# A hybrid SSD and attention layer: the first unit of the gate z directly behind the first B block, with four of its eight groups as seven products, and the sums of weight pairs begun with the constants

## The chip, the core and the metric

The kernel runs on one core of a Trainium2 chip. The metric is the device time of one execution in microseconds (us). The engines are called as in the profile: PE is TensorE's matmuls, PEld its weight loads, DVE is VectorE, ACT is ScalarE, POOL is GpSimd, SP is SyncE. A name with a q behind it (SPq, POOLq, ACTq) is the DMA queue that the engine feeds.

## The reference

One layer with S = 256 tokens and D = 2048 features, all in fp32. Only the first projection and what hangs on it matter here:

```python
u = rmsnorm(h, norm_mix_pre)
proj = einsum('bsd,de->bse', u, w_in)
z, xbc, dt_raw, q, k, v = split(proj, IN_SPLITS)      # 2048 | 4096 | 32 | 2048 | 2048 | 2048 columns
xbc = silu(causal_depthwise_conv(xbc, conv_w, conv_b))
xs, bm, cm = split(xbc, (2048, 2048 + 1024))          # X, B, C
dt = softplus(dt_raw + dt_bias)
y = ssd_chunked(xh, dt, a, bm, cm) + d_skip * xh      # 8 groups of 4 heads
yg = y * silu(z)                                      # z is needed here, at the end of a group
y_ssm = yg * rsqrt(mean(yg * yg) + EPS) * ssm_norm_w
y_att = ...                                           # dilated attention from q, k, v
h = h + rmsnorm(concat(y_ssm, y_att) @ w_out, norm_mix_post)
h = h + rmsnorm(relu(rmsnorm(h, norm_mlp_pre) @ w_up) ** 2 @ w_down, norm_mlp_post)
```

## The kernel before, in words

**Products.** Every fp32 operand is taken apart into a high part (ACT copies it rounded, L147) and a low part (DVE subtracts, L148). A product is then three matmuls: high by high, high by low, low by high. The 16 blocks of 128 features of the sum over D are taken in eight groups of two, k = 0 to 7. For 512 columns of weights one group is one load of 512 KB (`fetch`, L152, issued by SP into one of four buffers `raw`), one split of 128x1024 into `hi` and `lo` (five buffers each), and its matmuls.

**Two ways to multiply.** A *feature block* (`gemm_features`, L491: the blocks B, C and X, with queries and keys of the attention) puts 512 output features on the partitions: L485 multiplies the high parts of the weights by both parts of the activations, 512 wide, and L488 the low parts by the high parts of the activations, 256 wide. A *unit* (`unit`, L451: z, and later most of the kernel) has the tokens on the partitions, and takes two blocks of 512 columns and both token blocks together. A *plain group* of a unit (`row_tile`, L331 to L333) is 24 matmuls of 128x512. A *seven* (`seven`, L386) multiplies the 2x2 blocks of a group with seven products in place of eight, 21 matmuls (L418 to L420). For that it adds weight blocks: DVE makes three sums of 128x512 (L252), and ACT and DVE split seven blocks (three of 128x1024, one of 128x512). The activations' sums for a k are made once by `sums_of_acts` (L368): four operations on DVE (L377 to L380) and a split into two places of `sh` and `sl`. There are eight such places, for four values of k. After the last seven, `combine_new` (L422) folds the seven products' banks together, with four operations on DVE. Inside a seven the adds and splits keep the order of the code on ACT and DVE.

**Sums of pairs.** One addend of a seven comes summed from DRAM. `next_pair` (L270) issues on POOL a copy of one weight block to a place in DRAM (L279) and a second transfer that adds another block to it (L280); the first use of each of the five places is preceded by a tiny write (L278) from `room["pairs"]`, which sets when the chain may begin. SP fetches the sum later (L156) into half of a `raw`. Four pairs run ahead (`PAIRS_AHEAD`).

**The order of the work.** `first_block` (L577) makes the first B block by hand. The loop at L883 to L898 then calls, in this order, C0, X0, the first z unit (`gates(0)`, L779), X1, then B1, C1, X2, the second z unit, X3. What is put into `waiting` is carried on a step at each `pump`: `first_conv` (L742), which waits three pumps and then spreads the reciprocal norm over the partitions (`over_partitions`, L639: `dg` on DVE at L644, a matmul at L645, a copy `rbc` at L646) and does the convolution of B; `steps` (L663), which loads the weights of dt through ACT's queue (L665), splits them into `wdt`, sets `room["pairs"]` from `wdt` (L668), starts the first four pairs, and makes dt and its cumulative sums; and the SSD groups (L800). A unit's first seven drains `waiting` first (L462). The reciprocal norm `rstd` itself is a power on POOL (L142). At its end a block B, C or X empties its four banks through ACT (L508) and DVE (L509). A z unit takes all eight PSUM banks, four of them those of `acc`. The first z unit has sevens for k = 1 and 3 (the plan at L433; k = 7 comes last and is plain).

The constants `cst` are loaded by SP at L547, behind the last load of the first block. The instructions of each engine run in the order in which a scheduler has put them when the program was built; inside `high_priority` they may go ahead of what stands earlier in the code, as far as the buffers allow.

Of the kernel before, what the change touches and what calls it, by code (L numbers as in the profile page):

```python
# [10 lines left out]
F32 = mybir.dt.float32  # L11
# [32 lines left out]
AHEAD = 1_000_000  # L44
# [11 lines left out]
PAIRS_AHEAD = 4  # L56
# [21 lines left out]
def hymba_layer(ctx: ExitStack, tc: tile.TileContext, x, norm_mix_pre, w_in, conv_w, conv_b, dt_bias, a_log,  # L78
# [24 lines left out]
    def u(k):  # L103

        t, i = us[k]
        return t[:, i]
# [16 lines left out]
    cst = fp.tile([P, consts.shape[1] - P], F32, name="cst")  # L123
# [8 lines left out]
    def bank():  # L132
        return pacc.tile([P, NB], F32, name="acc")

    def psmall():
        return psm.tile([P, NB], F32, name="ps")
# [7 lines left out]
    def split(hi, lo, src, scale=None):  # L144

        if scale is None:
            return (nc.scalar.activation(hi, src, AF.Copy),  # L147
                    nc.vector.tensor_tensor(lo, src, hi.bitcast(F32), op=ALU.subtract))  # L148
        return (nc.scalar.activation(hi, src, AF.Copy, scale=scale),
                nc.vector.scalar_tensor_tensor(lo, src, scale, hi.bitcast(F32), op0=ALU.mult, op1=ALU.subtract))  # L150
# [27 lines left out]
    room = {}  # L178
# [75 lines left out]
    pairs = []  # L254

    w_z, w_v, w_ups, w_downs = w_in[:, COL_Z:], w_in[:, COL_V:], [w_up[:, hf * 4096:] for hf in range(2)], [w_down, w_down[4096:]]
    orders = {}

    def order_of(ks, by_seven):
        return [(k, k in by_seven) for k in ks]  # L260

    def blocks_of(n):
        return n if isinstance(n, tuple) else (n * NB, (n + 1) * NB)

    def plan(name, src, n, order, by_seven):

        orders[name, n] = order_of(order, by_seven)
        pairs.extend((src, blocks_of(n), k) for k in order if k in by_seven)

    def next_pair():  # L270

        if not pairs:
            return
        src, (ca, c), k = pairs.pop(0)
        cb = slice(c, c + NB)
        d = places[len(paired) % len(places)]
        if len(paired) < len(places):
            nc.gpsimd.dma_start(d[:, 0:1], room["pairs"])  # L278
        nc.gpsimd.dma_start(d, src[k * KB * P:(k * KB + 1) * P, cb])  # L279
        nc.gpsimd.dma_start(d, src[(k * KB + 1) * P:(k * KB + 2) * P, cb], accum_op=ALU.add)  # L280
        paired.append((src, ca, k, d))
# [148 lines left out]
            nc.vector.tensor_tensor(b[0], more[1], u, op=ALU.add)  # L430
            nc.vector.tensor_tensor(b[1], more[3], b[0], op=ALU.add)

    plan("z", w_z, 0, (0, 2, 4, 6, 1, 3, 5), (1, 3))  # L433
    plan("z", w_z, 2, (0, 2, 1, 4, 3, 6, 5), (1, 3, 5))
    qk_blocks = [(COL_Q + hb * NB, COL_K + hb * NB) for hb in range(3)]
    plan("qk", w_in, qk_blocks[1], (0, 2, 1, 4, 3, 5, 6), QK_SEVENS)
# [226 lines left out]
    def steps():  # L663
        raw = sp1.tile([P, NK, 32], F32, name="raw_dt")
        nc.scalar.dma_start(raw, w_in[:, COL_DT:COL_DT + 32].rearrange("(k p) n -> p k n", p=P))  # L665
        wdt = sp1.tile([P, NK, 64], F32R, name="wdt")
        split(wdt[:, :, 0:32], wdt[:, :, 32:64], raw)
        room["pairs"] = wdt[:, 0, 32:33].bitcast(F32)  # L668
        with tc.high_priority(offset=AHEAD):
            for _ in range(PAIRS_AHEAD):  # L670
                next_pair()
        yield
        yield
        acc = psmall()
        for k in range(NK):
            nc.tensor.matmul(acc[:64, :S], wdt[:, k], u(k)[:, 0], start=k == 0, stop=False)
            nc.tensor.matmul(acc[:64, :S], wdt[:, k], u(k)[:, 1], start=False, stop=k == NK - 1)
        both = sp1.tile([64, S], F32, name="both")
        nc.vector.tensor_copy(both, acc[:64, :S])
        yield  # L680
        p = psmall()
        for t in range(NT):
            nc.tensor.matmul(p[:, t * 32:(t + 1) * 32], both[:, t * P:(t + 1) * P], two[:64], start=True, stop=True)
        with tc.high_priority(offset=AHEAD):
            y = sp1.tile([P, NT, 32], F32, name="dt_y")
            for t in range(NT):
                nc.vector.scalar_tensor_tensor(y[:, t], p[:, t * 32:(t + 1) * 32], rstd[:, t:t + 1], bias_b,
                                               op0=ALU.mult, op1=ALU.add)

            e = sp1.tile([P, NT, 32], F32, name="dt_e")  # L690
            nc.vector.scalar_tensor_tensor(e, y, -1.0, y, op0=ALU.mult, op1=ALU.min)
            nc.scalar.activation(e, e, AF.Exp)
            r = sp1.tile([P, NT, 32], F32, name="dt_r")
            nc.vector.tensor_scalar(r, e, 2.0, None, op0=ALU.add)
            nc.vector.reciprocal(r, r)
            s = sp1.tile([P, NT, 32], F32, name="dt_s")
            nc.vector.tensor_mul(s, e, r)
            q = sp1.tile([P, NT, 32], F32, name="dt_q")
            nc.vector.tensor_mul(q, s, s)
            h = sp1.tile([P, NT, 32], F32, name="dt_h")  # L700
            nc.vector.tensor_scalar(h, q, 2.0 / 17, None, op0=ALU.mult)
            for n in (15, 13, 11, 9, 7, 5, 3):
                nc.vector.scalar_tensor_tensor(h, h, 2.0 / n, q, op0=ALU.add, op1=ALU.mult)
            nc.vector.scalar_tensor_tensor(h, h, 2.0, s, op0=ALU.add, op1=ALU.mult)
            nc.vector.scalar_tensor_tensor(dt, y, 0.0, h, op0=ALU.max, op1=ALU.add)
            ea = sp1.tile([P, 32], F32, name="dt_a")
            nc.scalar.activation(ea, a_b, AF.Exp)
        yield
        with tc.high_priority(offset=AHEAD):
            for t in range(NT):  # L710
                nc.vector.scalar_tensor_tensor(dA[:, t], dt[:, t], -1.0, ea, op0=ALU.mult, op1=ALU.mult)
        for _ in range(7):
            yield
        p = psmall()
        for t in range(NT):
            nc.tensor.matmul(p[:, t * 32:(t + 1) * 32], triu, dA[:, t], start=True, stop=True)
        nc.tensor.matmul(p[:, 64:96], ones, dA[:, 0], start=True, stop=True)
        nc.vector.tensor_copy(acs.rearrange("p t h -> p (t h)"), p[:, 0:64])
        nc.scalar.activation(eacs, acs[:, 1], AF.Exp)
        nc.vector.tensor_sub(toend, p[:, 64:96], acs[:, 0])  # L720
        nc.scalar.activation(toend, toend, AF.Exp)
        p = psmall()
        for t in range(NT):
            nc.tensor.matmul(p[:32, t * P:(t + 1) * P], dA[:, t], triu, start=True, stop=True)
        rowed = sp1.tile([32, S], F32, name="rowed")
        nc.vector.tensor_copy(rowed, p[:32, :S])
        nc.scalar.dma_start(acs_d, rowed)
# [37 lines left out]
    def place_of_sums():  # L765

        room["sum"] = mp.tile([P, 4, S], F32, name="cT", bufs=5).rearrange("p (k f) s -> p k (f s)", k=KB)
# [11 lines left out]
    def gates(n):  # L779

        room["own"] = deque(mp.tile([P, NT, NB], F32, name="tk", bufs=3)[:, t] for t in range(NT))
        place_of_sums()
        room["sums"] = [v[:, k:k + KB] for k in range(NK // 2, NK, KB) for v in (sh, sl)]
        room["raw"], room["turn"], room["acts"] = [], 0, act_u
        gated = [mp.tile([P, NT, NB], F32, name="tk", bufs=3) for _ in range(2)]

        def end(b):
            def at_end(t, a):
                with tc.high_priority(offset=AHEAD):
                    v = gated[b][:, t]  # L790
                    nc.vector.tensor_tensor(v, a, v, op=ALU.subtract if b else ALU.add)
                    nc.scalar.activation(v, v, AF.Silu, scale=rstd[:, t:t + 1])
            return at_end

        more = [psmall(), bank(), psmall(), bank()]
        unit(w_z, n, orders["z", n], (7,), [bank() for _ in range(2 * NT)], more,
             lambda x: combine_new([[v[:, t] for t in range(NT)] for v in gated], x), 0, (end(0), end(1)))
        return gated
# [85 lines left out]
    zs = []  # L884
    for hb in range(2):
        bT = conv_block(COL_B + hb * NB, 16 + 4 * hb, first if hb == 0 else None)
        if hb == 0:
            waiting.append(steps())
        cT = conv_block(COL_C + hb * NB, 24 + 4 * hb)
        for xb in (2 * hb, 2 * hb + 1):  # L890
            xT = conv_block(COL_X + xb * NB, 4 * xb)
            if xb % 2 == 0:
                zs += gates(xb)
            for j in range(2):
                g = 2 * xb + j
                waiting.append(ssd_group(sp, g, bT[:, g % 4], cT[:, g % 4], xT[:, 2 * j:2 * j + 2],
                                         zs[xb][:, :, j * 256:(j + 1) * 256]))
# [659 lines left out]
```

## Time and profile before

| | us |
|---|---|
| three runs | 1453.19, 1455.0, 1452.5 |
| their median | 1453.19 |
| the profiled execution: first to last instruction (span) | 1451.4 |
| median less span: what lies outside the span | 1.8 |
| PE busy in the span | 1442.4 |
| DVE busy | 1300.4 |
| ACT busy | 947.1 |
| POOL busy | 162.3 |

A row of a timeline gives the start in us, the busy time of the group in us, the engine, the line, the operation, output and inputs, their shapes and the count; what stands in square brackets is the idle time ahead of it and what ended it. In a list of waits the three numbers are the time in all, the count and the longest. In a list of DMA issues the last number is the median time from the issue to the landing. Lines (L488) are those of the kernel before; in the kernel after, lines behind L667 stand four lower up to the loop, and one higher behind it (L753 is L749 after).

### The profile page before, as it was taken

Reading aid. Unit: us, or ns where it says so; the run is one execution under the profiler, and the core shown is the slowest. Engines: PE = TensorE matmul, PEld = TensorE weight load, DVE = VectorE, ACT = ScalarE, POOL = GpSimd, SP = SyncE. Lnnn points to the kernel's source line nnn. Section 1 sums busy time; section 2 is a strip of 40 time slices with the busy share of each in tenths; the row PEclk is TensorE's granted clock in tenths of the full one; section 3 lists DMA queues with packets and bytes.
Section 4 is the critical chain, followed back from the end, with each engine's and each line's share of the span. In section 5 each row is a group of like instructions: output and inputs, shape, how many; then the busy total and the mean of one; then the engine's idle time right before and its main releaser. Section 6 shows DMA issues by size and latency. Waiting matters only on the chain.

```text
span 1451.4 us, 20394 instructions
## 1 busy us (share of the span) xinstructions
PE 1442.4 (99%) x7042; PEld 1214.7 (84%) x7042; DVE 1300.4 (90%) x1881; ACT 947.1 (65%) x1351; POOL 162.3 (11%) x244
## 2 busy tenths in 40 slices
PE   9999999999999999999999999999999999999998
PEld 8888888888888888888888888888888888888886
DVE  7788888988999788689988999999889999999998
ACT  7577669665666666556657677656465776766664
POOL 0201110131111000010100011010111110101000
PEclk9999999999999999999999999999999999999999
DMA  8977656756898658588976798688888888788854
GB/s 267 272 219 222 189 175 187 239 170 195 231 253 248 196 127 244 173 270 257 280 225 217 210 311 240 203 221 251 249 255 279 255 245 247 210 293 265 248 179 160
DMA packets 172359, 332.97 MB, mean 229 GB/s; under 512 B 16048, under 2 KB 18976, under 8 KB 172256
## 3 DMA queue, kind: packets, MB, share of 16 engines
q1 hardware_dynamic: 144736, 272.37, 58.1%
q0 software_dynamic: 19648, 45.63, 15.7%
q10 hardware_dynamic: 7872, 13.68, 2.8%
q8 instruction: 55, 0.90, 0.3%
q14 instruction: 48, 0.39, 0.1%
HBM read 327.39 MB, written 49.84 MB: 260 GB/s over the span
## 4 chain that ended last, share of the span: by engine, by line
PE 76%; ACT 1%; DVE 1%; DMA 0%; issue 0%; ACTq 0%
PE acc L331 10%; PE acc L333 10%; PE acc L332 10%; PE acc L418 7%; PE acc L419 7%; PE acc L420 7%; PE acc L485 4%; PE ps L331 3%; PE ps L332 3%; PE ps L333 3%; PE ps L418 2%; PE ps L419 2%; PE ps L420 2%; PE acc L488 2%; PE acc L1463 1%; PE ps L938 0%
## 5 line engine op out<-in xcount | busy, mean ns | idle before, releaser
L148 DVE TENSOR_TENSOR lo<-raw,hi 128x1024 fp32r<-128x1024 f32 (+1 forms) x387 | 470.1, 1220 | 79.1 <-ACT hi L147 76.3
L147 ACT ACTIVATE hi<-raw 128x1024 fp32r<-128x1024 f32 (+1 forms) x387 | 404.2, 1050 | 204.2 <-PE acc L333 71.4
L485 PE MATMUL acc<-ua,hi 128*128 128x512 f32 x520 | 141.2, 401 | 0.1
L147 ACT ACTIVATE hi<-e 128x1024 fp32r<-128x1024 f32 x66 | 70.2, 1063 | 68.5 <-DVE e L252 62.7
L485 PEld LDWEIGHTS acc<-ua,hi 128*128 128x128 f32 x520 | 91.3, 189 | 14.2 <-ACT hi L147 0.2
L331 PE MATMUL acc<-hi,ua 128*128 128x512 f32 x228 | 90.6, 397 | 0.0
L332 PE MATMUL acc<-lo,ua 128*128 128x512 f32 x228 | 89.3, 392 | 0.0
L333 PE MATMUL acc<-hi,ua 128*128 128x512 f32 x228 | 89.2, 391 | 0.0
L331 PE MATMUL acc<-hi,sh 128*128 128x512 f32 x220 | 86.9, 395 | 0.0
L333 PE MATMUL acc<-hi,sl 128*128 128x512 f32 x220 | 85.8, 390 | 0.0
L332 PE MATMUL acc<-lo,sh 128*128 128x512 f32 x220 | 85.7, 390 | 0.0
L488 PEld LDWEIGHTS acc<-ua,lo 128*128 128x128 f32 x520 | 76.5, 190 | 8.9
L148 DVE TENSOR_TENSOR lo<-e,hi 128x1024 fp32r<-128x1024 f32 x66 | 80.5, 1220 | 0.0
L488 PE MATMUL acc<-ua,lo 128*128 128x256 f32 x520 | 78.8, 282 | 0.0
L419 PE MATMUL acc<-lo,ah 128*128 128x512 f32 x180 | 70.1, 390 | 0.0
L420 PE MATMUL acc<-hi,al 128*128 128x512 f32 x180 | 70.1, 390 | 0.0
L418 PE MATMUL acc<-hi,ah 128*128 128x512 f32 x180 | 70.1, 390 | 0.0
L485 PE MATMUL acc<-uc,hi 128*128 128x512 f32 x208 | 61.4, 405 | 0.0
L148 DVE TENSOR_TENSOR lo<-ha,hi 128x1024 fp32r<-128x1024 f32 x43 | 52.5, 1221 | 6.0 <-ACT hi L147 5.8
L147 ACT ACTIVATE hi<-ha 128x1024 fp32r<-128x1024 f32 x43 | 45.2, 1057 | 19.4 <-PE acc L333 12.4
L147 ACT ACTIVATE hi<-r 128x512 fp32r<-128x512 f32 x66 | 41.5, 629 | 20.8 <-PE acc L333 8.8
L418 PE MATMUL acc<-hi,ua 128*128 128x512 f32 x137 | 53.7, 392 | 0.0
(572 smaller groups left out, 3722.3 us busy)
## 6 DMA issues: line engine op xcount, KB each, us to landing
raw<-in_w_in_dram SPq DMA_DIRECT2D x154, 512.0 KB, 4.5
raw<-in_w_down_dram SPq DMA_DIRECT2D x69, 512.0 KB, 5.7
raw<-in_w_up_dram SPq DMA_DIRECT2D x65, 512.0 KB, 4.8
raw<-in_w_out_dram SPq DMA_DIRECT2D x38, 512.0 KB, 5.1
raw<-pair SPq DMA_DIRECT2D x57, 256.0 KB, 4.3
pair<-in_w_up_dram POOLq DMA_DIRECT2D x56, 256.0 KB, 5.4
pair<-in_w_down_dram POOLq DMA_DIRECT2D x52, 256.0 KB, 6.3
pair<-in_w_in_dram POOLq DMA_DIRECT2D x42, 256.0 KB, 5.5
```

What stands on the lines that cost most here:

```text
L147: return (nc.scalar.activation(hi, src, AF.Copy), nc.vector.tensor_tensor(lo, src, hi.bitcast(F32), op=ALU.subtract))
L148: nc.vector.tensor_tensor(lo, src, hi.bitcast(F32), op=ALU.subtract))
L331: nc.tensor.matmul(dst[:, cs], a_h[:, r, ts], hi[:, j, cs], start=begin and j == 0, stop=False)
L332: nc.tensor.matmul(dst[:, cs], a_h[:, r, ts], lo[:, j, cs], start=False, stop=False)
L333: product[t] = nc.tensor.matmul(dst[:, cs], a_l[:, r, ts], hi[:, j, cs], start=False, stop=end and j == KB - 1)
L418: nc.tensor.matmul(dst, a_h, hi[:, j], start=own and first, stop=False)
L419: nc.tensor.matmul(dst, a_h, lo[:, j], start=False, stop=False)
L420: nc.tensor.matmul(dst, a_l, hi[:, j], start=False, stop=own and last)
L485: nc.tensor.matmul(acc[f], hi[:, j, f * P:(f + 1) * P], u(k0 + j), start=k0 + j == 0, stop=False, skip_group_check=True)
L488: nc.tensor.matmul(acc[f][:, 0], lo[:, j, f * P:(f + 1) * P], u(k0 + j)[:, 0], start=False, stop=k0 + j == NK - 1, skip_group_check=True)
L1463: nc.tensor.transpose(p[:, f * P:(f + 1) * P], r[:, f * P:(f + 1) * P], ident)
```

## The change

Three things are edited. The order of the first z unit is (0, 2, 4, 1, 3, 5, 6) with sevens for k = 1, 3, 5, 6, where it was (0, 2, 4, 6, 1, 3, 5) with sevens for k = 1 and 3. `gates(0)` is called directly behind the first B block, ahead of `steps`, C0 and X0. And the five tiny writes read one column of the constants instead of the dt weights, with the first four pairs begun ahead of that call.

```diff
-    plan("z", w_z, 0, (0, 2, 4, 6, 1, 3, 5), (1, 3))
+    plan("z", w_z, 0, (0, 2, 4, 1, 3, 5, 6), (1, 3, 5, 6))
...
         split(wdt[:, :, 0:32], wdt[:, :, 32:64], raw)
-        room["pairs"] = wdt[:, 0, 32:33].bitcast(F32)
-        with tc.high_priority(offset=AHEAD):
-            for _ in range(PAIRS_AHEAD):
-                next_pair()
         yield
...
         if hb == 0:
+            room["pairs"] = cst[:, 0:1]
+            with tc.high_priority(offset=AHEAD):
+                for _ in range(PAIRS_AHEAD):
+                    next_pair()
+            zs += gates(0)
             waiting.append(steps())
...
-            if xb % 2 == 0:
+            if xb == 2:
                 zs += gates(xb)
```

On POOL, at the program's start, before (`pad` belongs to the convolution of B, `rstd` is the reciprocal norm):

```order
L753 MEMSET pad 128x2x3 x2
L142 ISA
L142 TENSOR_TENSOR rstd<-rm,half 128x2
L278 DMA pair_89<-wdt 128x1
L278 DMA pair_90<-wdt 128x1
L278 DMA pair_91<-wdt 128x1
L278 DMA pair_92<-wdt 128x1
L278 DMA pair_93<-wdt 128x1
L279 DMA pair_89<-in_w_in_dram 128x512
```

And after, the same stretch from the last tiny write on:

```order
L278 DMA pair_93<-cst 128x1
L279 DMA pair_89<-in_w_in_dram 128x512
L279 DMA pair_90<-in_w_in_dram 128x512
L279 DMA pair_91<-in_w_in_dram 128x512
L279 DMA pair_92<-in_w_in_dram 128x512
L280 DMA pair_89<-in_w_in_dram 128x512
L280 DMA pair_90<-in_w_in_dram 128x512
L280 DMA pair_91<-in_w_in_dram 128x512
L280 DMA pair_92<-in_w_in_dram 128x512
L279 DMA pair_93<-in_w_in_dram 128x512
L749 MEMSET pad 128x2x3 x2
L280 DMA pair_93<-in_w_in_dram 128x512
```

The sums of the pairs now stand ahead of `pad` and of `rstd`, which follows behind the last row shown.

On DVE, from the last splits of the first block's end on, before (`raw`, `hi`, `lo` with numbers are buffers, `wdt` is the weights of dt):

```order
L148 TENSOR_TENSOR lo_598<-raw_595,hi_597 128x1024
L148 TENSOR_TENSOR lo_655<-raw_652,hi_654 128x1024
L148 TENSOR_TENSOR wdt_514<-raw_dt_512,wdt_514 128x16x32
L148 TENSOR_TENSOR lo_712<-raw_709,hi_711 128x1024
L148 TENSOR_TENSOR lo_802<-raw_799,hi_801 128x1024
L644 TENSOR_SCALAR dg_675<-ident_84,rstd_95 128x128
L644 TENSOR_SCALAR dg_678<-ident_84,rstd_95 128x128
```

And after, from the low part of the third plain group of z on (L252 are the adds of the first seven):

```order
L148 TENSOR_TENSOR lo_623<-raw_620,hi_622 128x1024
L252 TENSOR_TENSOR cT_478<-raw_644,raw_649 128x512
L148 TENSOR_TENSOR wdt_922<-raw_dt_920,wdt_922 128x16x32
L252 TENSOR_TENSOR cT_478<-cT_478,raw_649 128x512
L148 TENSOR_TENSOR lo_655<-raw_644,hi_654 128x1024
L252 TENSOR_TENSOR tk_477<-cT_478,raw_644 128x512
L148 TENSOR_TENSOR lo_660<-cT_478,hi_659 128x1024
L148 TENSOR_TENSOR lo_664<-raw_649,hi_663 128x1024
L644 TENSOR_SCALAR dg_562<-ident_84,rstd_95 128x128
L148 TENSOR_TENSOR lo_668<-tk_477,hi_667 128x512
```

The low part of `wdt` stood among splits of C's weights; it now stands between the first and the second add of the first seven, and the first `dg` behind that seven's third split.

On PE, around the matmuls of the reciprocal norm (L645), before, inside the C block:

```order
L488 MATMUL acc_466<-uc_78,lo_655 128x256 x2
L488 MATMUL acc_467<-uc_78,lo_655 128x256 x2
L645 MATMUL ps_674<-dg_675,ones_86 128x128
L645 MATMUL ps_674<-dg_678,ones_86 128x128
L485 MATMUL acc_464<-uc_78,hi_711 128x512 x2
```

And after, at the end of the third plain group of z and in its first seven:

```order
L332 MATMUL acc_486<-lo_623,ua_76 128x512
L645 MATMUL ps_561<-dg_562,ones_86 128x128
L333 MATMUL acc_486<-hi_622,ua_76 128x512
...
L420 MATMUL ps_481<-hi_654,ua_76 128x512
L645 MATMUL ps_561<-dg_565,ones_86 128x128
L418 MATMUL acc_485<-hi_654,ua_76 128x512
```

The two matmuls stood side by side in C; now one stands inside the last plain group ahead of the sevens and one inside the first seven. From the second B block on, PE's order is the same before and after.

## The prediction

> **What bounds the kernel now.** I read the page first, then the stages, then TensorE's timeline, then the waits.
>
> ```profile
> span 1451.4 us, 20394 instructions
> PE 1442.4 (99%) x7042; PEld 1214.7 (84%) x7042; DVE 1300.4 (90%) x1881; ACT 947.1 (65%) x1351; POOL 162.3 (11%) x244
> ```
>
> TensorE is busy for 99% of the span. Its ends are modelled, so I checked the distance from start to start. Here are the first matmul of the second group of seven in the first z unit, of the plain group behind it, and of the plain group after that:
>
> ```profile
> 110.27 0.39 PE L418 MATMUL ps<-hi,ua 128*128 128x512 f32 x1
> ...
> 115.03 0.39 PE L331 MATMUL acc<-hi,ub 128*128 128x512 f32 x1
> ...
> 120.47 0.39 PE L331 MATMUL acc<-hi,uc 128*128 128x512 f32 x1
> ```
>
> 21 matmuls take 4.76 us and 24 take 5.44: 0.227 us each in both, so nothing waits here. The waits of TensorE in the whole run are these:
>
> ```profile
> PE ps L1408 <- ACT dg L1407: 1.4, 1, 1.4
> PE ps L536 <- DVE half L525: 1.1, 1, 1.1
> PE ps L810 <- ACT bn L816: 0.6, 1, 0.6
> PE ps L566 <- DMA xs<-in_x_dram: 0.4, 1, 0.4
> PE acc L1160 <- DVE ha L1151: 0.2, 1, 0.2
> PE ps L845 <- DVE sl L150: 0.2, 1, 0.2
> ```
>
> They add up to 3.9 us. The kernel is a stream of matmuls, and a change gains only what it takes out of that stream. It can lose wherever VectorE (DVE) falls behind, since DVE is next (busy us and instructions of PE, PEld, DVE, ACT and POOL in stretches of 20 us, then the granted clock, the DMA share and GB/s):
>
> ```profile
> 20.00:40.00 20.00, 20.00 (x118) 17.40 (x117) 15.54 (x27) 16.17 (x33) 0.93 (x3) 1.00 0.72 216
> 40.00:60.00 20.00, 20.00 (x131) 18.09 (x129) 11.78 (x18) 8.54 (x11) 6.79 (x12) 1.00 0.90 279
> 80.00:100.00 20.00, 20.00 (x97) 16.66 (x97) 18.67 (x36) 15.10 (x26) 1.68 (x5) 1.00 0.68 215
> 100.00:120.00 20.00, 20.00 (x90) 16.56 (x89) 17.43 (x22) 17.93 (x31) 1.48 (x3) 1.00 0.81 208
> ```
>
> With two sevens the old place of z (84 to 126 us) already has DVE at 17.4 to 18.7 of 20. The new place (33 to 75 us) has it at 15.5 and 11.8, so there is room on average.
>
> **The change part by part.** *Fewer products.* Two plain groups become sevens: 2 x (5.44 - 4.76) = 1.36 us less on TensorE. That is 0.09%, below the 0.2% (2.9 us) that a measurement of this kernel can tell from no change.
>
> *More on DVE.* The rows for its prices are these; the first is a 128x512 operation, the second a low part of 128x1024:
>
> ```profile
> 73.93 0.69 DVE L754 TENSOR_TENSOR pad<-cT,rbc 128x512 f32<-128x512 f32 x1
> 74.53 1.22 DVE L148 TENSOR_TENSOR lo<-raw,hi 128x1024 fp32r<-128x1024 f32 x1
> 75.67 1.67 DVE L761 SCALAR_TENSOR_TENSOR cT<-pad,cw,cT 128x256 f32<-128x256 f32 x4
> ```
>
> From start to start 0.60 and 1.14 us. A seven costs DVE three adds, three low parts of 1024 and one of 512: 4 x 0.60 + 3 x 1.14 = 5.8 us against 4.76 us of TensorE. A plain group costs 2.3 against 5.44. Before, two sevens stood together, with plain groups around them. Now four stand in a row, so DVE must be 4 us ahead when they begin. Between them also stand the activations' sums for k = 5 and 6 (the first used to be made in the second z unit). The cover is DVE's lead, and a lead needs data that is there early.
>
> *The sums of pairs.* Their start moves from the dt weights to the constants. The old chain, and the landings:
>
> ```profile
> 46.80 2.91 POOL L278 DMA_DIRECT2D pair<-wdt  x5 [7.12 <-DVE wdt L148]
> 55.92 0.88 POOL L280 DMA_DIRECT2D pair<-in_w_in_dram  x1 [2.58 <-DMA pair<-in_w_in_dram]
> ```
> ```profile
> 18.75 0.43 SPq L547 DMA_DIRECT2D cst<-in_consts_dram  x1
> ```
> ```profile
> cst<-in_consts_dram SPq DMA_DIRECT2D x1, 272.0 KB, 4.7
> pair<-in_w_in_dram POOLq DMA_DIRECT2D x42, 256.0 KB, 5.5
> raw<-pair SPq DMA_DIRECT2D x57, 256.0 KB, 4.3
> ```
>
> The constants land at 18.75 + 4.7 = 23.4. The first accumulating transfer goes out 55.92 - 46.80 = 9.1 us later, at 32.6, and lands about 5.5 us after that, at 38.1; SyncE then fetches the sum, which is in SBUF at about 42.5. Nothing is queued ahead of it on POOL; behind it there waits rstd, which comes up below.
>
> *The dt weights.* In the new DVE order their low part stands between the two adds of the first seven, and on ACT their high part stands ahead of that seven's second split:
>
> ```profile
> 36.23 0.39 ACTq L665 DMA_DIRECT2D raw_dt<-in_w_in_dram  x1
> 45.12 0.63 ACT L147 ACTIVATE wdt<-raw_dt 128x512 fp32r<-128x512 f32 x1 [2.66 <-DMA raw_dt<-in_w_in_dram]
> 45.79 0.69 DVE L148 TENSOR_TENSOR wdt<-raw_dt,wdt 128x512 fp32r<-128x512 f32 x1 [2.07 <-ACT wdt L147]
> ```
>
> ACT issues this transfer behind the same six splits as before, so DVE can't pass it before 45.8. Before, only plain C products stood behind it. Now the whole run of sevens does, and DVE is in order. That is the step on which my forecast rests: the later of 42.5 (pair) and 45.8 (dt weights) is 45.8.
>
> *DVE from there.* From the low part of wdt to the low part of the last product of the fourth seven the new order has 12 low parts of 1024 (13.7 us), 20 operations of 512 (12.0) and 11 small ones, which I take at 0.25 (2.8), after rows like these:
>
> ```profile
> 49.02 0.48 DVE L644 TENSOR_SCALAR dg<-ident,rstd 128x128 f32<-128x128 f32 x2
> 57.54 0.42 DVE L646 COPY rbc<-ps 128x256 f32<-128x256 f32 x1
> ```
>
> 28.5 us, so it ends at 74.3, and TensorE two matmuls later at 74.8. Without a wait TensorE would be there earlier. The old C block starts here:
>
> ```profile
> 32.61 0.71 PE L485 MATMUL acc<-ua,hi 128*128 128x512 f32 x2
> ```
>
> From 32.6, three plain groups and four sevens are 72 + 84 matmuls, 35.4 us, and the two matmuls of the reciprocal norm among them 0.2: 68.2. The wait is 74.8 - 68.2 = 6.6 us. Three smaller waits vanish in it. z takes the four banks of the B block, which are free only after ACT's copies and DVE's adds:
>
> ```profile
> 32.50 1.19 ACT L508 ACTIVATE cT<-acc 128x256 f32<-128x256 f32 x4
> 33.17 1.41 DVE L509 TENSOR_TENSOR cT<-acc,cT 128x256 f32<-128x256 f32 x4
> ```
>
> Each of the four adds takes 1.41 / 4 = 0.35 us, so z's first matmul, which needs the first bank back, starts at about 33.6, 1.0 us late; C took two spare banks first. The two matmuls for the norm (L645) stand in TensorE's order before and inside the first seven, and wait for DVE operations behind three splits of that seven; TensorE reaches the first at about 48.3 and DVE at 51. rstd, on POOL, comes behind the fifth pair's second transfer, by the old spacing near 47, in time for that. The last plain group and C find their low parts ready by the same count (75.8 and 78.1, needed at 75.7 and 78.3).
>
> *Later.* C, X and the next X lose nothing by average: a feature block asks DVE for eight low parts, 9.1 us of 22. The first two SSD groups now follow X's convolution directly; the last two of them paid 0.6 and 0.2 us in the waits above, so I add 0.3. From the second B block on TensorE's order is that of before.
>
> The sum is -1.4 + 6.6 + 0.3 = +5.5 us. The profiled span is 1451.4 us and the median of the runs 1453.2, so 1.8 us lie outside the span and stay: span 1456.9, time 1458.7.
>
> **The rivals.** *The lead holds* (not slower). If the dt weights and the pair are there by the time DVE is free, it starts the first add at about 41, after the sixth low part:
>
> ```profile
> 39.67 1.23 DVE L148 TENSOR_TENSOR lo<-raw,hi 128x1024 fp32r<-128x1024 f32 x1 [0.79 <-ACT hi L147]
> ```
>
> Then 0.6 + 28.5 us end at 70.0, the wait is 2.3 and the sum +1.2, or 1454.4; if DVE's small operations cost less and nothing waits, -1.4, or 1451.8. For it: in the old unit DVE still had to wait for ACT in the second seven. Against it: the transfer of raw_dt took 8.9 us. It decides when that transfer and the pair land before about 42.5.
>
> ```profile
> 108.07 1.23 DVE L148 TENSOR_TENSOR lo<-raw,hi 128x1024 fp32r<-128x1024 f32 x1 [2.34 <-ACT hi L147]
> ```
>
> *The sums crowd the loads* (slower still). By queue, and by stage where they now run:
>
> ```profile
> q1 hardware_dynamic: 144736, 272.37, 58.1%
> q0 software_dynamic: 19648, 45.63, 15.7%
> ```
> ```profile
> 35.00:40.00 5.00, 5.00 (x28) 4.30 (x27) 4.16 (x8) 3.32 (x6) 0.93 (x3) 1.00 0.88 236
> 40.00:45.00 5.00, 5.00 (x31) 4.44 (x30) 2.12 (x2) 1.06 (x1) 0.00 (x0) 1.00 1.05 337
> ```
>
> A load of 512 KB takes 0.581 x 1451.4 / 272.37 x 0.524 = 1.62 us of all 16 engines and a half of a pair's sum 1.31. Eight halves are 10.5 us, and seven loads 11.3: 21.8 us between 23.4 and 45.1, with raw_dt still to come. If raw_dt and the pair slip by 3.7 us, to 49.5, the sum is +9.2: 1462.4. The rows leave it open, because fewer raws are fetched meanwhile: SyncE stops at the pair. The Trainium skill (Trainium Kernel Development and Optimization, Key Constraints) speaks against this change here: it says that transfers issued from SP, ACT and POOL all run on the same 16 engines and interleave. By that rule the sum is the 1462.4 of this rival, by the old landings 1458.7.
>
> *Faster.* The 1.4 us and every wait of the list would make 5.3 us, or 1447.9. But those waits stand at the start, at 319 to 330 us and at the end, where no order changes.
>
> **How the numbers follow.** DVE held at the dt weights: 0.57 (43 to 48 us for their arrival, 1455.9 to 1460.9). The lead holds: 0.25 (1451.8 to 1455). Crowding: 0.13 (to 1464). Faster: 0.05. Slower by over 0.2% (above 1456.1) is 0.57 + 0.13 = 0.70, within 0.25, faster 0.05. The range 1453.0 to 1463.0 leaves out the low end of the second case, the fourth, and the high end of the third.
>
> **What would show it.** In the profile after: wdt's low part on DVE at 45 to 47 us, with the adds of the first seven around it; TensorE waiting at the first L645 for DVE for 2 to 3 us, and again in the third and fourth seven at low parts; the first z unit ending near 80 us instead of 73.5; the same length as before from 210 us on. Wrong would be: no wait of TensorE between 33 and 80 us (the lead held), waits for DMA rather than DVE (crowding), or a wait of over 1 us in the first two SSD groups.

## The result, and the profile after

The changed kernel takes 1471.14 us (median of 4 runs, 1468.2 to 1472.2) where the kernel before takes 1453.16 (1452.5 to 1455.0): a ratio of 1.0119, with a 95% interval of 1.0105 to 1.0134. The forecast was 1458.7 with a range up to 1463.0, so the direction was right and the size was not: the loss is 18 us where 5.5 were expected. The profiled execution took 1470.52 us, with a span of 1468.6; that is 17.2 more than the 1451.4 before.

The waits of TensorE, in the list of waits of the changed kernel (us in all, count, longest):

```profile
PE ps L645 <- DVE dg L644: 12.0, 1, 12.0
PE ps L419 <- DVE lo L148: 1.9, 1, 1.9
...
PE ps L841 <- DVE sl L150: 1.1, 2, 0.8
...
PE ps L679 <- DVE both L675: 0.6, 1, 0.6
```

The wait stands where the prediction put it, at the first matmul of the spread norm, with DVE named as the releaser. It is 12.0 us in place of the 2 to 3 that were foreseen. DVE's timeline tells what DVE itself was waiting for:

```profile
41.65 1.23 DVE L148 TENSOR_TENSOR lo<-raw,hi 128x1024 fp32r<-128x1024 f32 x1
49.04 0.69 DVE L252 TENSOR_TENSOR cT<-raw 128x512 f32<-128x512 f32 x1 [6.16 <-DMA raw<-pair]
54.13 0.69 DVE L148 TENSOR_TENSOR wdt<-raw_dt,wdt 128x512 fp32r<-128x512 f32 x1 [4.39 <-ACT wdt L147]
54.73 0.69 DVE L252 TENSOR_TENSOR cT<-cT,raw 128x512 f32<-128x512 f32 x1
...
59.35 0.28 DVE L644 TENSOR_SCALAR dg<-ident,rstd 128x128 f32<-128x128 f32 x1
...
64.91 0.42 DVE L646 COPY rbc<-ps 128x256 f32<-128x256 f32 x1 [2.46 <-PE ps L645]
...
84.25 0.68 DVE L148 TENSOR_TENSOR lo<-tk,hi 128x512 fp32r<-128x512 f32 x1
```

Two landings hold it, both late. The first sum of a pair is in SBUF at 49.0 (the prediction had 42.5), and the dt weights pass DVE at 54.1 (it had 45.8). What DVE then does was costed right: from 54.13 to the end of the last low part (84.25, and 0.60 from start to start), are 30.7 us, of which 2.46 are a wait for TensorE, so 28.3 of work; the prediction had 28.5. ACT's timeline shows the transfer behind it:

```profile
38.72 1.06 ACT L147 ACTIVATE hi<-raw 128x1024 fp32r<-128x1024 f32 x1 [2.54 <-DMA raw<-in_w_in_dram]
38.88 0.39 ACTq L665 DMA_DIRECT2D raw_dt<-in_w_in_dram  x1
...
53.46 0.63 ACT L147 ACTIVATE wdt<-raw_dt 128x512 fp32r<-128x512 f32 x1 [6.58 <-DMA raw_dt<-in_w_in_dram]
```

It is issued 2.7 us later than before (38.88 against 36.23), because the split ahead of it on ACT waits for z's weights, and it takes 14.6 us in place of 8.9. Meanwhile the sums run, on POOL:

```profile
22.84 2.86 POOL L278 DMA_DIRECT2D pair<-cst  x5 [22.39 <-DMA cst<-in_consts_dram]
28.25 2.10 POOL L279 DMA_DIRECT2D pair<-in_w_in_dram  x4 [2.55 <-DMA pair<-cst]
33.19 1.72 POOL L280 DMA_DIRECT2D pair<-in_w_in_dram  x2 [2.83 <-DMA pair<-in_w_in_dram]
...
50.38 1.01 POOL L142 TENSOR_TENSOR rstd<-rm,half 128x2 f32<-128x2 f32 x1
```

The first accumulating transfer goes out at 33.2, near the forecast 32.6. SyncE's fetch of that sum, which waits for its landing, goes out at 42.9:

```profile
42.91 0.34 SPq L156 DMA_DIRECT2D raw<-pair  x1
```

So the sum took 9.7 us in place of 5.5, and its fetch 6.1 (42.91 to 49.0) in place of 4.3. `rstd` is made at 50.4, where the prediction had 47, but DVE comes to `dg` only at 59.35, so that cost nothing here. By stage (busy us of PE, PEld, DVE, ACT, POOL, then the granted clock, the DMA share, GB/s), the kernel before from 30 to 50 us, and the changed kernel from 30 to 70:

```profile
30.00:40.00 10.00, 10.00 (x57) 8.56 (x56) 8.27 (x14) 8.32 (x17) 0.93 (x3) 1.00 0.78 221
40.00:50.00 10.00, 10.00 (x63) 8.96 (x62) 6.08 (x9) 5.60 (x6) 3.19 (x6) 1.00 0.78 237
```

```profile
30.00:40.00 10.00, 10.00 (x50) 8.25 (x48) 6.46 (x10) 7.35 (x16) 4.40 (x8) 1.00 1.02 291
40.00:50.00 10.00, 7.64 (x34) 6.01 (x32) 3.39 (x6) 2.13 (x2) 0.27 (x1) 1.00 1.12 303
50.00:60.00 10.00, 0.32 (x1) 0.32 (x2) 5.87 (x8) 3.15 (x4) 4.18 (x6) 0.54 0.75 150
60.00:70.00 10.00, 10.00 (x38) 8.16 (x38) 7.54 (x15) 5.26 (x6) 1.36 (x2) 0.78 0.59 169
```

From 30 to 50 us the DMA share is 1.02 and 1.12, where it was 0.78, and DVE, the engine that the forecast counted, is busy for 6.5 and 3.4 of 10. And after the wait the clock is down: 0.78 from 60 to 70 us. TensorE's timeline has the slow matmuls one by one:

```profile
59.68 0.80 PE L645 MATMUL ps<-dg,ones 128*128 128x128 f32 x2 [12.04 <-DVE dg L644]
60.13 0.77 PE L333 MATMUL acc<-hi,ua 128*128 128x512 f32 x1
60.70 0.63 PE L331 MATMUL acc<-hi,ua 128*128 128x512 f32 x1
61.13 0.63 PE L332 MATMUL acc<-lo,ua 128*128 128x512 f32 x1
```

From 60.70 on they stand 0.43 us apart in place of 0.227, until 64.1.

### The profile page after: what moved, and what is told of

Same layout as the page of the kernel before. It is cut to its first block, busy times and chain, and to the rows that moved or that the text cites. A ratio compares the mean times of both kernels' runs of the same rounds, so it can differ in the third digit from the quotient of the medians.

```text
span 1468.6 us, 20422 instructions
## 1 busy us (share of the span) xinstructions
PE 1444.8 (98%) x7036; PEld 1214.9 (83%) x7036; DVE 1308.2 (89%) x1896; ACT 952.7 (65%) x1358; POOL 164.5 (11%) x248
## 4 chain that ended last, share of the span: by engine, by line
PE 75%; ACT 1%; DVE 1%; DMA 0%; issue 0%; ACTq 0%
PE acc L333 10%; PE acc L331 10%; PE acc L332 10%; PE acc L420 6%; PE acc L419 6%; PE acc L418 6%; PE acc L485 4%; PE ps L333 3%; PE ps L332 3%; PE ps L331 3%; PE ps L418 2%; PE ps L420 2%; PE ps L419 2%; PE acc L488 2%; PE acc L1464 1%; PE ps L939 0%
## 5 line engine op out<-in xcount | busy, mean ns | idle before, releaser
L147 ACT ACTIVATE hi<-ha 128x1024 fp32r<-128x1024 f32 x43 | 45.2, 1057 | 17.6 <-PE acc L333 10.4
```

The source lines that it names most:

```text
L147: return (nc.scalar.activation(hi, src, AF.Copy), nc.vector.tensor_tensor(lo, src, hi.bitcast(F32), op=ALU.subtract))
```

## The experiments

The ratios are against the kernel before, with 95% intervals; they are worked out over all runs and are not the quotient of two medians.

| kernel | z's place | sevens | sums begin | median us | ratio |
|---|---|---|---|---|---|
| changed | behind B0 | 4 | constants | 1471.14 | 1.0119 [1.0105, 1.0134] |
| sums early only | behind X0 | 2 | constants | 1460.37 | 1.0049 [1.0036, 1.0062] |
| half of the sums early | behind X0 | 2 | two with constants | 1453.20 | 1.0003 [0.9994, 1.0011] |
| sums early, dt weights ahead | behind X0 | 2 | constants | 1452.81 | 1.0000 [0.9991, 1.0009] |
| four sevens only | behind X0 | 4 | dt weights | 1457.14 | 1.0033 [1.0022, 1.0044] |
| two sevens | behind B0 | 2 | constants | 1469.86 | 1.0117 [1.0103, 1.0131] |
| dt split late | behind B0 | 4 | constants | 1467.58 | 1.0103 [1.0089, 1.0117] |
| dt weights ahead | behind B0 | 4 | constants | 1468.97 | 1.0114 [1.0099, 1.0130] |
| dt weights and norm ahead | behind B0 | 4 | constants | 1464.56 | 1.0083 [1.0069, 1.0097] |
| the same, two sevens | behind B0 | 2 | constants | 1466.32 | 1.0081 [1.0067, 1.0095] |
| the same, two sevens, half of the sums | behind B0 | 2 | two with constants, the rest with rstd | 1461.65 | 1.0056 [1.0043, 1.0068] |
| no sums in z's first unit | behind B0 | 4 | none early | 1462.60 | 1.0063 [1.0047, 1.0080] |

**The parts alone.** The theory after the result: the early sums share the DMA engines with the loads, the dt weights land late, and DVE, in order, stands behind them. The rivals: z's place costs by itself, or the four sevens do. First the sums alone, at the old place.

```diff
-        room["pairs"] = wdt[:, 0, 32:33].bitcast(F32)
-        with tc.high_priority(offset=AHEAD):
-            for _ in range(PAIRS_AHEAD):
-                next_pair()
...
         if hb == 0:
+            room["pairs"] = cst[:, 0:1]
+            with tc.high_priority(offset=AHEAD):
+                for _ in range(PAIRS_AHEAD):
+                    next_pair()
             waiting.append(steps())
```

> The kernel before, with only the sums of pairs begun with the constants, ahead of C0; z stays behind X0 with two sevens. Theory, the early sums crowd the loads: raw_dt lands near 53 instead of 45, so the dt products (and C's low parts behind them on DVE) hold TensorE for some 7 us in C0: 1460 (1457 to 1464). Rival, the place of z is what costs, and the sums' early begin costs nothing by itself: 1453 (1452 to 1454.5).

1460.37. The list of waits of this kernel names the dt weights, where C's block multiplies them:

```profile
PE ps L672 <- DVE wdt L148: 6.6, 1, 6.6
```

So one of the three edits, alone, costs some 7 us (0.0049 x 1453), with z still at its old place behind X0. The landing of the dt weights follows the number of sums that run beside it. The transfers between 20 and 56 us (count, size, median us to landing), before, with half of the sums early, and with all:

```profile
raw_dt<-in_w_in_dram ACTq DMA_DIRECT2D x1, 256.0 KB, 8.9
```
```profile
raw_dt<-in_w_in_dram ACTq DMA_DIRECT2D x1, 256.0 KB, 10.8
```
```profile
raw_dt<-in_w_in_dram ACTq DMA_DIRECT2D x1, 256.0 KB, 16.9
```

The half was this edit against the kernel with all sums early, with the other two pairs begun with the dt weights as before:

```diff
             room["pairs"] = cst[:, 0:1]
             with tc.high_priority(offset=AHEAD):
-                for _ in range(PAIRS_AHEAD):
+                for _ in range(2):
                     next_pair()
```

> As the run with the early sums at the old place, with two of the four pairs begun with the constants and the other two with the dt weights as before. Theory, shared DMA engines: half the sums are half the delay, so the dt weights land near 49 to 50 in place of 54.6 and TensorE waits 1.5 to 3 us at the dt products: 1455.5 (1453.5 to 1457.5). Rival, the delay comes from something that any early sum brings (POOL's place, a queue's order): as with four, 1460.

1453.20, no difference, and 0.3 us below the expected range: the split of the dt weights on DVE at 47.85 still comes before this kernel's first product with them, at 49.07. The landing moved by 2 us, but nothing was waiting for it yet. Then the dt weights were put ahead of the sums:

```diff
+        for half_of, place in enumerate((rbc, rbq)):
+            rs = slice(half_of * D // 2, (half_of + 1) * D // 2)
+            nc.scalar.dma_start(place.rearrange("p (k n) -> p k n", n=32),
+                                w_in[rs, COL_DT:COL_DT + 32].rearrange("(k p) n -> p k n", p=P))
...
-        raw = sp1.tile([P, NK, 32], F32, name="raw_dt")
-        nc.scalar.dma_start(raw, w_in[:, COL_DT:COL_DT + 32].rearrange("(k p) n -> p k n", p=P))
```

> As the run with the early sums at the old place (z behind X0, two sevens, sums begun with the constants), and the dt weights are loaded behind the constants' loads on ACT's queue, ahead of the sums, in two halves into memory that is free until the norm is spread. Theory: the 7.6 us of that run were the dt weights' late landing alone, so TensorE's wait at the dt products (6.6 us) goes: 1453.5 (1452 to 1455). Rival, the sums delay the loads of C's weights as well, and the wait only moves to C's products: 1456 or more.

1452.81, as expected. All that the early sums cost at the old place was the late landing of this one load.

**Four sevens alone.** The kernel before with the new order of z's first unit.

```diff
-    plan("z", w_z, 0, (0, 2, 4, 6, 1, 3, 5), (1, 3))
+    plan("z", w_z, 0, (0, 2, 4, 1, 3, 5, 6), (1, 3, 5, 6))
```

> The kernel before, with only the order of the first z unit changed: sevens for k = 1, 3, 5, 6. Place and begin of the sums as before. Theory: this part alone costs little, since raw blocks and sums run ahead there; between -1.4 us (the products saved) and +3 (DVE 17.4 to 18.7 of 20 us busy there, and four sevens in a row ask 4 us more of it than TensorE takes): 1454 (1451.8 to 1456). Rival, the four sevens are what costs: 1459 or more.

1457.14: 1 us past the expected range, between it and the rival. The waits and the stage:

```profile
PE acc L418 <- ACT hi L147: 2.2, 3, 1.2
PE ps L419 <- DVE lo L148: 1.6, 1, 1.6
```
```profile
110.00:120.00 10.00, 6.59 (x26) 4.46 (x25) 9.63 (x15) 9.97 (x19) 1.36 (x2) 1.00 0.80 177
```

DVE is busy for 9.6 and ACT for 10.0 of 10 us. I had priced DVE alone; four sevens in a row fill ACT as well. The saving of 1.4 us in products is more than given back.

**Two sevens at the new place.** The changed kernel with the old order (the same line, turned back).

> The changed kernel with the old order of the first z unit: four plain groups, then sevens for k = 1 and 3. The move and the early sums stay. Theory, late transfers (crowded by the early sums) hold DVE at the dt weights until 54: TensorE again waits some 11 us at the first L645 matmul (dg stands behind the dt weights, two low parts and two adds), but DVE has time to make it good afterwards; no 1.4 us are saved. 1467 (1464 to 1469). Rival, DVE has too much work in four sevens: 1453 to 1456.

1469.86, 0.9 us above the expected range's end and far from the rival: taking two sevens away gains next to nothing while the transfers are late. The wait at the norm is 10.4 us in this kernel's list.

**The dt weights at the new place.** First only their split was moved:

```diff
+        with ExitStack() as order:
+            for last in late:
+                order.enter_context(tc.issue_after(last.ins))
-        split(wdt[:, :, 0:32], wdt[:, :, 32:64], raw)
+            split(wdt[:, :, 0:32], wdt[:, :, 32:64], raw)
```

where `late` holds the last add and the last split of the last seven.

> The changed kernel, with the split of the dt weights (high part on ACT, low part on DVE) put behind the last seven of the first z unit; their transfer stays where it was. Theory, DVE held by the dt weights: in the changed kernel DVE made its first add at 49.0 us and could only go on at 54.1. Now it goes on when the raw blocks are there, at 50.0; the first dg then comes near 54.6 in place of 59.4 and TensorE waits about 7 us at the first L645 matmul in place of 12. The two dg stand next to each other in the new order, so the wait for rbc (2.5 us) goes too. Some 6 us faster than the changed kernel: 1465 (1463 to 1467). Rival, the raw blocks and sums themselves come late: no more than 1 us gained, 1470. Rival, the norm's matmuls hold TensorE by their place: rstd is only made at 50.4 to 51.4 us, so at best 8 us of the wait go: 1463.

1467.58, 0.6 us above the expected range. The wait at the norm is 7.2 us, as expected, but 2.3 us came back at the dt products, which were now late, so the gain was 3.6 and not 6 (the profiled execution, 1470.33, was the slowest of four). Then the load and the split were both put ahead (the diff above, with the split ahead of `gates(0)`):

> The changed kernel with only the dt weights loaded and split ahead (not the norm, whose dg now stands behind the second seven's splits on DVE). Theory: DVE makes its first add when the first sum is fetched, at 47 to 48 us in place of 49.0, and goes on at once in place of at 54.7; the 12 us at the norm's matmuls become some 4, but DVE stays the bound of the four sevens: 1466 (1463 to 1468). Rival, the dt weights were the whole loss: 1453 to 1456. Rival, they were none of it: 1470.

1468.97. The wait at the norm is gone from the list, and others have come up:

```profile
PE acc L419 <- DVE lo L148: 4.0, 4, 2.1
PE acc L418 <- ACT hi L147: 2.4, 2, 1.7
PE ps L841 <- POOL xdd L824: 2.0, 2, 1.6
```

DVE made its first add at 48.7, when the sum had been fetched. The time is 1 us above the expected range, and by itself (1467.4 to 1470.9) it can't be told from the rival's 1470; it is the list that tells them apart. So the dt weights were the last to arrive, and not the only ones late. Next the norm was put ahead too (`rstd` before the fifth pair on POOL, its spreading before the first seven's adds on DVE):

```diff
+            if len(paired) >= PAIRS_AHEAD:
+                order.enter_context(tc.issue_after(early.ins))
...
+             ready=lambda: line.update(dve=spread[0]))
```

> The changed kernel (z behind the first B block, four sevens), with the dt weights loaded ahead of the sums and split before z, rstd made ahead of the fifth pair on POOL, and the spread norm put ahead of the first seven's adds on DVE. Only the sums' own landing (48 to 49 us) and DVE's work for four sevens are left. Theory: TensorE waits 0 to 1 us for the norm, then for the sevens' low parts; DVE begins near 49 and needs 27 us to the last low part, so TensorE is some 9 us behind the 68.2 us it would need, less the 1.4 us of products: 1460.5 (1458 to 1463). Rival, the dt weights and the norm were all of the loss: 1452 to 1454.

1464.56, 1.6 us above the range: its list has 2.1 us for `xdd` in the first SSD groups, which the theory did not have. And the sevens now wait for ACT more than for DVE's low parts:

```profile
PE acc L422 <- ACT hi L147: 3.8, 2, 2.1
```

And with the old order of z:

> As the run with dt weights and norm ahead at the new place, with the old order of four plain groups and two sevens (k = 1 and 3). Theory: TensorE reaches the first seven at 54.4 us, where DVE, from 49 on, has its low parts ready, and two sevens leave DVE time; up to 3 us at the norm's matmuls, whose dg stands behind the fourth group's low part: 1454.5 (1453 to 1457). So the place of z by itself would cost nothing. Rival, z's place costs by itself (banks of B, order of later blocks): 1459 or more.

1466.32, a clear miss (the runs lie between 1462.7 and 1466.8, and the profiled one is the slowest). All four sums begin early in this kernel too, so it neither bears out nor refutes my claim that the place by itself costs nothing. Its list of waits:

```profile
PE ps L656 <- DVE dg L655: 5.4, 1, 5.4
PE ps L847 <- POOL xdd L830: 2.0, 2, 1.6
...
PE ps L847 <- DVE sl L150: 0.8, 2, 0.6
```

and DVE's timeline ahead of the first of them:

```profile
49.14 1.22 DVE L148 TENSOR_TENSOR lo<-raw,hi 128x1024 fp32r<-128x1024 f32 x1 [2.33 <-ACT hi L147]
50.28 0.47 DVE L655 TENSOR_SCALAR dg<-ident,rstd 128x128 f32<-128x128 f32 x2
```

`dg` stands behind the low part of z's fourth plain group, and those weights, an ordinary load, were late too. If the sums are the reason, they delay the ordinary loads of that stage too. To see whether that is so, only the two sums that this unit needs were begun early:

```diff
             room["pairs"] = cst[:, 0:1]
             with tc.high_priority(offset=AHEAD):
-                for _ in range(PAIRS_AHEAD):
+                for _ in range(2):
                     next_pair()
+            room["pairs"] = rstd[:, 0:1]
+            with tc.high_priority(offset=AHEAD), tc.issue_after(early.ins):
+                for _ in range(PAIRS_AHEAD - 2):
+                    next_pair()
```

> As the run with dt weights and norm ahead and two sevens at the new place, with only the two pairs that this unit needs begun with the constants; the other pairs begin when rstd is made. Theory, shared DMA engines: the weights of z's fourth plain group land near 44 in place of 47.9 us, so dg comes near 47 in place of 50.3 and TensorE's wait at the norm's matmuls falls from 5.4 us to 1.5 to 2.5, with no slow matmuls behind it; the 3.3 us of waits in the first two SSD groups stay: 1459 (1457 to 1461). Rival, the place costs what it costs whatever is transferred: 1466.

1461.65, 0.7 us above the range. The waits:

```profile
PE ps L656 <- DVE dg L655: 2.2, 1, 2.2
PE ps L847 <- POOL xdd L830: 2.0, 2, 1.6
```

The wait at the norm fell from 5.4 to 2.2 us, and the one for `xdd` stayed. But `dg` did not come near 47:

```profile
48.92 0.47 DVE L655 TENSOR_SCALAR dg<-ident,rstd 128x128 f32<-128x128 f32 x2
```

That is 1.4 us sooner than 50.28. The rest of the 3.2 us is TensorE's: in the profiled execution the first block itself ended late, at

```profile
34.49 0.27 PE L563 MATMUL ps<-ident,rows 64*128 64x64 f32 x1
```

against 32.67 in the kernel with all four sums and 32.33 before. No edit of this kernel accounts for it; the timeline shows where it comes from: from 7.08 us four matmuls of 128x512 take 1.85 us, where the kernel before takes 1.00, and by 13.4 us TensorE is 2.2 us behind. So this profile alone doesn't separate the sums from the late start. The times do speak for the sums: all five runs lie between 1459.2 and 1462.8, those with all four sums between 1462.7 and 1466.8.

**No sums at all.** Last, the changed kernel with z's first unit left without sums: a plain weight block is fetched in the sum's place, so that the addition in DRAM is left out. The sums of the later units begin with the dt weights, as in the kernel before. DVE and TensorE keep the changed kernel's order in z.

```diff
+        if src is w_z and ca == 0:
+            return src[k * KB * P:(k * KB + 1) * P, NB:2 * NB]
...
+        if (name, n) != ("z", 0):
+            pairs.extend((src, blocks_of(n), k) for k in order if k in by_seven)
```

> The changed kernel without the first z unit's sums of pairs: SP fetches one weight block where it fetched the sum, so nothing is transferred for sums before the dt weights are there (the sums of the later units begin with the dt weights, as in the kernel before). The addition in DRAM is left out of this unit's sevens. The order of the instructions on DVE and TensorE in z is that of the changed kernel. Theory: with the transfers uncrowded the dt weights land near 45 again, DVE goes on from 45.8 and the prediction's own sum holds: 1458.7, up to 2.5 us more where the first SSD groups wait: 1460 (1457.5 to 1462). Rival, the place and the four sevens cost as much without any sums in the way: 1467 to 1471. Rival, the late transfers were all of it: 1452 to 1455.

1462.60 (1457.5 to 1467.0, the widest spread of all), just above the expected range. DVE:

```profile
45.45 0.69 DVE L148 TENSOR_TENSOR wdt<-raw_dt,wdt 128x512 fp32r<-128x512 f32 x1 [2.27 <-ACT wdt L147]
...
50.67 0.33 DVE L647 TENSOR_SCALAR dg<-ident,rstd 128x128 f32<-128x128 f32 x1
...
55.48 0.42 DVE L649 COPY rbc<-ps 128x256 f32<-128x256 f32 x1 [1.71 <-PE ps L648]
```

With the sums gone, DVE passes the dt weights at 45.45 and makes `dg` at 50.67, where the prediction had 45.8 and 51. So by the medians 1471.1 - 1462.6 = 8.5 us of the loss are the sums' transfers. The other 9.4 stand against the 5.5 of the prediction: the wait at the norm is 3.3 us in this kernel's list and the one at a low part 1.9, together 5.2 where the prediction had 6.6; what it had not priced are two stretches of slow matmuls (52.3 to 55.7 and 72.9 to 76.3 us), which by TensorE's starts cost about 3.5 us.

## Why the prediction was right and wrong

- **Slower, at the dt weights, with DVE held in order: right.** The wait came at the first L645 matmul, as named.
- **When they land: wrong, and this step made the size.** The prediction took both landings from the kernel before: "the later of 42.5 (pair) and 45.8 (dt weights) is 45.8". They were 49.0 and 54.1. The whole sum rested on landings that were measured without the traffic that the change adds to the same stage. The rival "The sums crowd the loads" was the true case; its slip of 3.7 us, for which the prediction shows no working, should have been 8.3 (54.13 - 45.79), which by the prediction's own sum gives 1458.7 + 8.3 = 1467.0, and its chance of 0.13 was far too low. The rule of the Trainium skill that was cited there (Trainium Kernel Development and Optimization, Key Constraints) is that all queues share the 16 engines. The traces agree with it: 8.9, 10.8 and 16.9 us for the same transfer with none, half and all of the sums. Whether it is the engines or the memory behind them that is full, no run here separates.
- **How to tell the cases apart: wrong.** I wrote that waits for DMA rather than DVE would mean crowding. TensorE's list names DVE, ACT's names the DMA; the releaser of a wait is the last link of a chain, and it has to be followed back.
- **DVE's work of 28.5 us: right** (28.3).
- **The bank wait of 1.0 us between B and z: wrong.** z's first matmul starts at 32.61 in the changed kernel, right behind the transposes of the parameters; in the forecast this term was absorbed by the longer wait, so it did no harm.
- **What was missing: the price of a wait behind its end.** The prediction put it at nothing. TensorE's timeline has 2.1 us of slow matmuls behind the wait: eight at 0.43 - 0.227 = 0.2 us, and 0.5 at the first and the last. DVE waits 2.46 us for `rbc`, for which it needs TensorE's second L645, behind those matmuls; so they hold up DVE as well, which makes TensorE wait again at 79 us. How much of the time these two cost by themselves was not tried.
- **"Later", 0.3 us: too small, and at another place.** The list has 0.6 behind the dt products (L679) and 0.8 at an SSD group at 207 us; the first two groups, for which the 0.3 was meant, don't wait in the changed kernel. In five other kernels of the new place they wait 2.0 us for `xdd`. The length of the earlier wait doesn't tell which: two sevens has 10.4 us at the norm and pays, the run without sums has 3.3 and doesn't. What these five share is the order on DVE, which makes `xdt` of both groups side by side, as in dt weights and norm ahead with two sevens,

```profile
154.65 2.26 DVE L828 TENSOR_TENSOR xdt<-xs,dt 128x256 f32<-128x256 f32 x4
```

where the changed kernel makes them 3.9 us apart:

```profile
156.50 0.75 DVE L822 TENSOR_TENSOR xdt<-xs,dt 128x256 f32<-128x256 f32 x2
...
160.41 0.75 DVE L822 TENSOR_TENSOR xdt<-xs,dt 128x256 f32<-128x256 f32 x2
```

- **From the second B block on nothing changes: right.** The tail is the same but for the shift, which is 17.7 us at 320 us and 17.3 at the end.

The ledger of the profiled execution, from TensorE's starts: 12.2 at the norm and 0.3 at that matmul itself, 2.1 of slow matmuls, 2.05 at the seven's low part (79.2 us), 0.8 at the dt products and 1.0 in the SSD groups are 18.45; less 1.36 for the products, 17.1, against 17.2 measured. Three things stay open. What the place of z costs by itself is not shown: no run has z behind the first B block with two sevens and no sums beside it. That the order of `xdt` on DVE is what costs the 2.0 us was not tried. And the spread of the last experiment is not explained. No version beat the kernel before: the best, with early sums and the dt weights ahead, is equal to it within 0.1%.

## What to carry to other kernels

A landing time read from a trace holds for the traffic of that trace: when a change starts transfers earlier, every load of that stage has to be priced again, first the one behind which an engine stands in order. Here the DMA share of the stage was 0.78 already, and transfers that cost the compute engines nothing were not free for the loads. And when one wait is mended, expect the next late thing to show: here the dt weights, the sums, ACT's splits, z's own weights and the SSD groups came up one behind the other.

## What the runs showed of the hardware

TensorE's clock is lost in a wait, and not in every one. Behind waits of 12.0, 7.2 and 5.4 us (the changed kernel, the dt split late, dt and norm ahead with two sevens) the next wide matmuls stood 0.43 us apart. The stretch lasted from 60.1 to 64.1, from 54.9 to 56.7 and from 51.5 to 56.3 us: it does not grow with the wait. Shorter waits went both ways. In the kernel with the dt weights ahead, waits of 2.1 and 0.8 us close behind each other were followed by a slow stretch from 53.1 to 58.8 us; the 2.2 us of the half of the sums at the new place were not. One of 2.05 us (from TensorE's starts; 1.9 in the list) in the run without sums was followed by a slow stretch, and one of 2.05 us in the changed kernel was not; the granted clock (0.83 and 1.00, the third number from the end) in the stage that holds the first, and in the one that holds the second:

```profile
70.00:80.00 10.00, 8.11 (x29) 6.36 (x29) 8.71 (x12) 7.17 (x10) 0.00 (x0) 0.83 0.70 184
```
```profile
80.00:90.00 10.00, 8.49 (x38) 6.96 (x39) 10.00 (x13) 7.41 (x10) 0.00 (x0) 1.00 0.78 224
```

The Trainium skill (TensorE: Matmul & The Clock Gate, What's actually happening) has half rate after an idle window of about 3.4 us, with a window that runs freely. The long waits agree with it. A wait of 2.05 us is shorter than that window, and the clock was lost behind it all the same; there the measurement decides. Whether a run meets such a stretch may be part of the spread of the run without sums (1457.5 to 1467.0, mean clocks of 0.999 and 0.995 in those two).
